# Parting one tile's load so that its last 448 columns go to four of the sixteen DMA engines

## The chip, the cores and the metric

The kernel runs on one core of a Trainium2 chip. The metric is the device time of one execution in microseconds (us). Executions of one kernel agree within some 0.3% as a rule; now and then one is more than 1.5% above the fastest and counts as "slow". A *ratio* below is the mean time of one kernel's fast runs over the mean time of the other's fast runs of the same rounds on the same chip, so it is not quite the ratio of the medians that are quoted beside it.

## The reference

A softmax over groups of 544 neighbouring columns, in float32. The input is 285.2 MB and the output as much.

```python
# x: (4, 4096, 4352) float32, 8 groups of 544 columns
x_g = x.reshape(B, N, G, Dg)
x_g = x_g - x_g.max(axis=-1, keepdims=True)
exp = np.exp(x_g)
out = exp / exp.sum(axis=-1, keepdims=True)
```

## The kernel before

The 16,384 rows make 64 tiles of 128 partitions with two rows each, so a tile is 128 x 8,704 float32, and one partition's row of it is 34,816 B. There are six buffers in SBUF, the on-chip memory. A tile is loaded, its 16 group maxima are taken on DVE (the vector engine), ACT (the scalar engine) computes the exponentials with their sums, DVE takes the reciprocals and scales in place, and the tile is stored from the same buffer. SP (the sync engine) issues the loads, POOL (GpSimd) most of the stores, and a load into a used buffer waits for the store of six tiles earlier:

```python
    for t in range(nt):
        if t >= NT:
            nc.sync.wait_ge(stored[t % NT], 16 * (t // NT))
        tile_in = bufs[t % NT]
        if t < nt - 1:
            nc.sync.dma_start(out=tile_in[:, :], in_=xt[t]).then_inc(landed[t % NT], 16)
        else:
            # ... the last tile (63) is loaded in two halves of columns
    for t in range(nt - LAST, nt):      # LAST = 2: SP also stores tiles 62 and 63
        nc.sync.wait_ge(scaled, t + 1 if t < nt - 1 else len(parts))
        nc.sync.dma_start(out=ot[t], in_=bufs[t % NT][:, :]).then_inc(last_stored, 16)

    for t in range(nt - LAST):          # POOL stores the others
        nc.gpsimd.wait_ge(scaled, t + 1)
        nc.gpsimd.dma_start(out=ot[t], in_=bufs[t % NT][:, :]).then_inc(stored[t % NT], 16)
```

DVE works in a fixed order, in which the max of a tile stands ahead of the scale of the tile before.

```python
    vector_max(0)                       # waits for landed[...]
    for n in range(len(parts)):
        if n + 1 < len(parts):
            vector_max(n + 1)
        vector_scale(n)                 # waits for the exponentials of n
```

Of the kernel before, what the change touches and what calls it, by code (L numbers as in the profile page):

```python
# [1 line left out]

# [4 lines left out]


@with_exitstack
def kernel(  # L10
    ctx: ExitStack,
    tc: tile.TileContext,
    x: bass.AP,
    out: bass.AP,
):
    nc = tc.nc
    G = 8
    P = 128
    R = 2
    NT = 6  # L20
    RG = R * G
    xf = x.flatten_outer_dims()
    of = out.flatten_outer_dims()
    N, D = xf.shape
    Dg = D // G
    nt = N // (P * R)
    LAST = 2
    FIRST = 2
    turns = (nt - 1 - FIRST) // NT
    f32 = mybir.dt.float32  # L30
    X = mybir.AxisListType.X
    Exp = mybir.ActivationFunctionType.Exp
    xt = xf.rearrange("(t p r) d -> t p (r d)", p=P, r=R)
    ot = of.rearrange("(t p r) d -> t p (r d)", p=P, r=R)

    landed = [tc.alloc_semaphore(f"landed{b}") for b in range(NT)]
    stored = [tc.alloc_semaphore(f"stored{b}") for b in range(NT)]
    last_landed = tc.alloc_semaphore("last_landed")
    last_stored = tc.alloc_semaphore("last_stored")


    max_done = tc.alloc_semaphore("max_done")
    exp_done = tc.alloc_semaphore("exp_done")
    rec_done = tc.alloc_semaphore("rec_done")
    scaled = tc.alloc_semaphore("scaled")

    ctx.enter_context(tc.tile_critical(  # L47
        sync_engine=mybir.EngineType.Pool, no_gpsimd_drain=True))
    bufs = [ctx.enter_context(nc.sbuf_tensor(f"xt{b}", [P, R * D], f32)) for b in range(NT)]
    mx = ctx.enter_context(nc.sbuf_tensor("mx", [P, NT, RG], f32))  # L50
    sm = ctx.enter_context(nc.sbuf_tensor("sm", [P, NT, RG], f32))
    rs = ctx.enter_context(nc.sbuf_tensor("rs", [P, NT, RG], f32))

    parts = [(t, slice(0, RG)) for t in range(nt - 1)]
    parts += [(nt - 1, slice(r * G, (r + 1) * G)) for r in range(R)]

    def groups(t, g):
        return bufs[t % NT][:, :].rearrange("p (g d) -> p g d", d=Dg)[:, g, :]

    def vector_max(n):  # L60
        t, g = parts[n]
        i = nc.vector.reduce_max(  # L62
            out=mx[:, t % NT, g], in_=groups(t, g), axis=X, negate=True)
        if g.start == 0:
            i.wait_op(landed[t % NT], 16 * (t // NT + 1), "sem-ge")
        else:
            i.wait_op(last_landed, 16, "sem-ge")
        i.then_inc(max_done, 1)

    def vector_scale(n):  # L70
        t, g = parts[n]
        nc.vector.reciprocal(out=rs[:, t % NT, g], in_=sm[:, t % NT, g]).wait_op(  # L72
            exp_done, n + 1, "sem-ge").then_inc(rec_done, 1)
        xg = groups(t, g)
        nc.vector.tensor_tensor(  # L75
            out=xg,
            in0=xg,
            in1=rs[:, t % NT, g].unsqueeze(2).to_broadcast([P, g.stop - g.start, Dg]),
            op=mybir.AluOpType.mult,
        ).wait_op(rec_done, n + 1, "sem-ge").then_inc(scaled, 1)  # L80

    def scalar_exp(n, count):
        t, gs = parts[n]
        xg = groups(t, gs)
        for g in range(gs.start, gs.stop):
            i = nc.scalar.activation(  # L86
                out=xg[:, g - gs.start, :],
                in_=xg[:, g - gs.start, :],
                func=Exp,
                bias=mx[:, t % NT, g:g + 1],  # L90
                scale=1.0,
                accum_out=sm[:, t % NT, g:g + 1],
            )
            if g == gs.start:
                i.wait_op(max_done, count, "sem-ge")
        i.then_inc(exp_done, 1)



    for t in range(nt):  # L100
        if t >= NT:
            nc.sync.wait_ge(stored[t % NT], 16 * (t // NT))
        tile_in = bufs[t % NT]
        if t < nt - 1:
            nc.sync.dma_start(out=tile_in[:, :], in_=xt[t]).then_inc(landed[t % NT], 16)  # L105
        else:
            for r in range(R):
                nc.sync.dma_start(
                    out=tile_in[:, r * D:(r + 1) * D], in_=xt[t, :, r * D:(r + 1) * D],
                ).then_inc(landed[t % NT] if r < R - 1 else last_landed, 16)  # L110
    for t in range(nt - LAST, nt):
        nc.sync.wait_ge(scaled, t + 1 if t < nt - 1 else len(parts))
        nc.sync.dma_start(out=ot[t], in_=bufs[t % NT][:, :]).then_inc(last_stored, 16)


    for t in range(nt - LAST):
        nc.gpsimd.wait_ge(scaled, t + 1)
        nc.gpsimd.dma_start(out=ot[t], in_=bufs[t % NT][:, :]).then_inc(stored[t % NT], 16)  # L118
    for t in range(nt - NT, nt - LAST):
        nc.gpsimd.wait_ge(stored[t % NT], 16 * (t // NT + 1))  # L120
    nc.gpsimd.drain()
    nc.gpsimd.wait_ge(last_stored, 16 * LAST)

    nc.scalar.preload_act_table(Exp)  # L124

    for n in range(FIRST):
        scalar_exp(n, n + 1)
    nc.scalar.sem_inc(max_done, -FIRST)
    with nc.scalar.Fori(0, turns):
        for k in range(NT):  # L130
            scalar_exp(FIRST + k, k + 1)
        nc.scalar.sem_inc(max_done, -NT)
    for k, n in enumerate(range(FIRST + turns * NT, len(parts))):
        scalar_exp(n, k + 1)


    vector_max(0)
# [3 lines that stand above are left out]
        vector_scale(n)  # L141


# [1 line left out]
_INS = ['x']  # L145
_OUTS = [((4, 4096, 4352), 'float32')]


# [23 lines left out]
```

## Time and profile before

| | before |
|---|---|
| median of the runs | 1326.43 us (1326.30 to 1326.44) |
| span in the profile | 1324.7 us |
| moved | 570.48 MB at 431 GB/s |
| DVE / ACT busy | 90% / 57% |

The prediction below shows the main lines of the page and of the timeline. Beside them, the table by stretches from 1220 to 1320 us is of use. Its columns are the stretch, its length, the busy time of DVE, ACT and POOL with the count of their instructions, a clock that is of no interest here, the busy share of the 16 DMA engines, and GB/s.

```profile
1220.00:1260.00 40.00, 35.95 (x7) 23.63 (x64) 1.07 (x2) 1.00 1.00 430
1260.00:1280.00 20.00, 19.97 (x4) 11.82 (x32) 0.53 (x1) 1.00 1.01 433
1280.00:1300.00 20.00, 19.56 (x6) 11.14 (x31) 0.00 (x0) 1.00 1.01 436
1300.00:1320.00 20.00, 4.90 (x2) 0.78 (x3) 0.00 (x0) 1.00 0.99 427
```

The DMA engines are fully busy to the very end, also after DVE has finished at 1305.7 us: the last stores still wait in line. The times to landing of the two stores that SP issues (minimum, median, maximum) say the same:

```profile
L113 SPq DMA_DIRECT2D out_dram<-xt x2: 343/346/348, 1290.2 to 1305.8; - x2
...
DMA to landing us min/median/max: 17.5/20.1/22.8
```

The last store, issued at 1305.8 us, needs 17.5 us although its rows take only 10.3 us: it stands behind the rows of tile 62.

### The profile page before, as it was taken

Reading aid. Unit: us, or ns where it says so; the run is one execution under the profiler, and the core shown is the slowest. Engines: PE = TensorE matmul, PEld = TensorE weight load, DVE = VectorE, ACT = ScalarE, POOL = GpSimd, SP = SyncE. Lnnn points to the kernel's source line nnn. Section 1 sums busy time; section 2 is a strip of 40 time slices with the busy share of each in tenths; the row PEclk is TensorE's granted clock in tenths of the full one; section 3 lists DMA queues with packets and bytes.
Section 4 is the critical chain, followed back from the end, with each engine's and each line's share of the span. In section 5 each row is a group of like instructions: output and inputs, shape, how many; then the busy total and the mean of one; then the engine's idle time right before and its main releaser. Section 6 shows DMA issues by size and latency. Waiting matters only on the chain.

```text
span 1324.7 us, 2465 instructions
## 1 busy us (share of the span) xinstructions
DVE 1190.0 (90%) x195; ACT 757.4 (57%) x2049; POOL 33.3 (3%) x66
## 2 busy tenths in 40 slices
DVE  5999999988989889898898998988989889898893
ACT  3765566547456465564655646556465474654751
POOL 0000000000000000000000000000000000000000
DMA  9999999999999999999999999999999999999998
GB/s 404 421 434 433 432 432 434 434 432 431 435 435 432 430 434 437 432 432 432 436 434 430 433 435 433 431 433 435 433 433 431 434 436 432 431 432 437 432 432 372
DMA packets 18582, 570.48 MB, mean 431 GB/s; under 512 B 2064, under 2 KB 2064, under 8 KB 2064
## 3 DMA queue, kind: packets, MB, share of 16 engines
q1 hardware_dynamic: 9648, 294.13, 51.5%
q0 software_dynamic: 8928, 276.30, 48.3%
q14 instruction: 6, 0.05, 0.0%
HBM read 285.21 MB, written 285.21 MB: 431 GB/s over the span
## 4 chain that ended last, share of the span: by engine, by line
another core or an unknown queue 69%; DVE 20%; DMA 7%; ACT 1%; SPq 1%; issue 0%; POOLq 0%
DVE xt L75 10%; DVE mx L62 10%; DMA out_dram<-xt 4%; DMA xt<-in_x_dram 3%; ACT xt L86 1%; SPq L105 1%; DVE rs L72 0%; SPq L167 0%; POOLq L47 0%; POOLq L156 0%
## 5 line engine op out<-in xcount | busy, mean ns | idle before, releaser
L86 ACT ACTIVATE xt<-xt,mx 128x544 f32<-128x544 f32 x1024 | 750.1, 734 | 542.4 <-DVE mx L62 542.4
L62 DVE TENSOR_REDUCE mx<-xt 128x16 f32<-128x8704 f32 (+1 forms) x65 | 590.1, 9079 | 110.8 <-DMA xt<-in_x_dram 110.8
L75 DVE TENSOR_TENSOR xt<-xt,rs 128x8704 f32<-128x8704 f32 (+1 forms) x65 | 590.6, 9086 | 2.2
L86 ACT ACTIVATION_READ_ACCUMULATOR xt<-xt,mx 128x1 f32 x1024 | 191.6, 187 | 0.0
L118 POOL DMA_DIRECT2D out_dram<-xt x62 | 33.1, 534 | 1243.5 <-DVE xt L75 1243.5
L72 DVE RECIPROCAL rs<-sm 128x16 f32<-128x16 f32 (+1 forms) x65 | 15.7, 242 | 2.8 <-ACT xt L86 2.8
L124 ACT ACT_TABLE_LOAD x1 | 1.3, 1283 | 0.9 <-PEq L156 0.9
L156 POOL MEMSET const-float32-0.0<- 128x1 f32 x1 | 0.1, 98 | 0.2 <-issue 0.2
L156 POOL MEMSET const-bfloat16-1.0<- 128x1 bf16 x1 | 0.1, 101 | 0.0
L156 POOL MEMSET const-uint8-127<- 128x1 uint8 x1 | 0.1, 99 | 0.0
L156 POOL MEMSET const-float32-1.0<- 128x1 f32 x1 | 0.1, 98 | 0.0
## 6 DMA issues: line engine op xcount, KB each, us to landing
xt<-in_x_dram SPq DMA_DIRECT2D x63, 4352.0 KB, 32.4
out_dram<-xt POOLq DMA_DIRECT2D x62, 4352.0 KB, 51.5
out_dram<-xt SPq DMA_DIRECT2D x2, 4352.0 KB, 20.1
xt<-in_x_dram SPq DMA_DIRECT2D x2, 2176.0 KB, 35.1
```

What stands on the lines that cost most here:

```text
L62: i = nc.vector.reduce_max(out=mx[:, t % NT, g], in_=groups(t, g), axis=X, negate=True)
L72: nc.vector.reciprocal(out=rs[:, t % NT, g], in_=sm[:, t % NT, g]).wait_op(exp_done, n + 1, "sem-ge").then_inc(rec_done, 1)
L75: nc.vector.tensor_tensor(out=xg, in0=xg, in1=rs[:, t % NT, g].unsqueeze(2).to_broadcast([P, g.stop - g.start, Dg]), op=mybir.AluOpType.mu ...
L86: i = nc.scalar.activation(out=xg[:, g - gs.start, :], in_=xg[:, g - gs.start, :], func=Exp, bias=mx[:, t % NT, g:g + 1], scale=1.0, accum ...
L105: nc.sync.dma_start(out=tile_in[:, :], in_=xt[t]).then_inc(landed[t % NT], 16)
L118: nc.gpsimd.dma_start(out=ot[t], in_=bufs[t % NT][:, :]).then_inc(stored[t % NT], 16)
L124: nc.scalar.preload_act_table(Exp)
L156: nc = _bacc.Bacc("TRN2", target_bir_lowering=False, num_devices=1)
```

## The change

The load of tile 61 is parted. The main DMA takes all but the last 448 columns of all 128 partitions. Two more DMAs take those columns for 124 and for 4 partitions. 124 and 4 look chosen because each runs on four engines, where 128 partitions run on 16: the prediction cites the rule for this. The intent, as far as the code tells it, is to take a little work off twelve engines and to give it to four. The wait of the max of tile 61 counts two more DMAs.

```diff
+    PARTED, COL, RANGES = 61, R * D - 448, [124, 4]
@@ vector_max
         if g.start == 0:
-            i.wait_op(landed[t % NT], 16 * (t // NT + 1), "sem-ge")
+            more = 16 * len(RANGES) if t >= PARTED and t % NT == PARTED % NT else 0
+            i.wait_op(landed[t % NT], 16 * (t // NT + 1) + more, "sem-ge")
@@ the loads
-        if t < nt - 1:
+        if t == PARTED:
+            nc.sync.dma_start(out=tile_in[:, :COL], in_=xt[t, :, :COL]).then_inc(
+                landed[t % NT], 16)
+            p = 0
+            for size in RANGES:
+                nc.sync.dma_start(
+                    out=tile_in[p:p + size, COL:], in_=xt[t, p:p + size, COL:],
+                ).then_inc(landed[t % NT], 16)
+                p += size
+        elif t < nt - 1:
             nc.sync.dma_start(out=tile_in[:, :], in_=xt[t]).then_inc(landed[t % NT], 16)
```

## The prediction

> **What bounds the kernel now.** I read the page first (engine shares, the 40 slices, the DMA queues), then the DMA issues, the waits of the DMA queue, the chain of work that ended last, the timeline of DVE, POOL and SP over the last 130 us, and last the trace's single packet records. The page and the waits of SP:
>
> ```profile
> DVE 1190.0 (90%) x195; ACT 757.4 (57%) x2049; POOL 33.3 (3%) x66
> DMA  9999999999999999999999999999999999999998
> GB/s 404 421 434 433 432 432 434 434 432 431 435 435 432 430 434 437 432 432 432 436 434 430 433 435 433 431 433 435 433 433 431 434 436 432 431 432 437 432 432 372
> q1 hardware_dynamic: 9648, 294.13, 51.5%
> q0 software_dynamic: 8928, 276.30, 48.3%
> ...
> SPq L105 <- DMA out_dram<-xt: 1201.7, 57, 67.8
> ```
>
> The reader is to see that the DMA is full from the first slice to the last, at some 433 GB/s: 570.4 MB at that rate are 1317 us of the 1324.7 us span. Loads are on q1 (issued by SP, line 105), stores on q0 (issued by POOL, line 118), and SP's only large wait is for a store to free a buffer. DVE, at 90%, is next. In the steady part a tile takes 20.6 us and DVE works 18.6 us of them (max 9.1, reciprocal 0.2, scale 9.2, gaps), so its slack is 2 us a tile. The timeline shows this for tiles 60 to 63, with the stores of tiles 58 to 61 beside it:
>
> ```profile
> 1214.59 0.53 POOL L118 DMA_DIRECT2D out_dram<-xt  x1 [20.07 <-DVE xt L75]
> 1235.21 0.53 POOL L118 DMA_DIRECT2D out_dram<-xt  x1 [20.10 <-DVE xt L75]
> 1255.82 0.53 POOL L118 DMA_DIRECT2D out_dram<-xt  x1 [20.08 <-DVE xt L75]
> 1276.47 0.53 POOL L118 DMA_DIRECT2D out_dram<-xt  x1 [20.11 <-DVE xt L75]
> ...
> 1216.28 9.22 DVE L62 TENSOR_REDUCE mx<-xt 128x16 f32<-128x8704 f32 x1 [1.99 <-DMA xt<-in_x_dram]
> 1236.89 9.22 DVE L62 TENSOR_REDUCE mx<-xt 128x16 f32<-128x8704 f32 x1 [1.97 <-DMA xt<-in_x_dram]
> 1246.30 9.22 DVE L75 TENSOR_TENSOR xt<-xt,rs 128x8704 f32<-128x8704 f32 x1
> 1257.54 9.22 DVE L62 TENSOR_REDUCE mx<-xt 128x16 f32<-128x8704 f32 x1 [2.01 <-DMA xt<-in_x_dram]
> 1290.22 15.90 SPq L113 DMA_DIRECT2D out_dram<-xt  x2
> ```
>
> The max at 1236.89 is that of tile 61 and waits for its load. DVE's program has max(61) ahead of scale(60), so a late tile 61 also holds back the store of tile 60, issued at 1255.82. After max(62) at 1257.54 DVE waits for no more loads: from there the tail is a chain of DVE work up to the last store's issue (the second of line 113, 1305.78 by its record), and the rows of that store run 10.3 us on every engine.
>
> **The packet records.** One row of a tile (34,816 B) is one record, and each DMA engine takes one after the other without a gap, so the 16 engines can be threaded by matching ends to starts. One engine's thread around the load of tile 63, which comes in half rows (start us, queue, bytes):
>
> ```
> 1255.74 q1 17408    1256.39 q0 34816
> 1257.67 q1 17408    1258.32 q0 34816
> 1259.60 q1 17408    1260.25 q0 4
> 1260.25 q1 17408    1260.90 q0 34816
> ```
>
> Two things follow. Cost: a whole row holds the engine 1.285 us, a half row 0.645 us, so a record costs about 5 ns plus 36.8 ns per 1000 B. Order: the engine alternates between q0 and q1 **record by record, whatever their size**. A half row waits a full store row for its turn, and even the 4-byte semaphore record at the end of a DMA uses up a turn. The engines' last records end between 1319.8 and 1322.8 us, 14 of the 16 by 1321.5.
>
> **What the Trainium skill says.** "DMA: Bandwidth & Descriptors", section "Why a DMA increments its semaphore by 16 and not by 1": a DMA uses the largest k up to 16 that divides the outer dimension, on the lowest-numbered engines if issued from SP. 124 and 4 both give k = 4; 31 rows and 1 row on each of engines 0 to 3. The trace before has only k = 16 and cannot confirm it. Same page, "Queues, rings and completion order": an engine round-robins between queues at packet granularity, of some 9 to 17 descriptors. The trace agrees with the turns but not the size: here a turn is one row. Same page, "Rules for kernel authors": a smaller k confines a DMA to fewer engines.
>
> **The change, part by part.**
> 1. The main load of tile 61 has rows of 33,024 B: 8 rows times 1,792 B times 36.8 ns/KB = 0.53 us less work on every engine.
> 2. Engines 0 to 3 get 32 rows of 1,792 B, each 5 + 66 = 71 ns: 2.28 us more, net +1.75 us. Were throughput all, the end would move by -0.5 us (the two latest engines not among the four: they end 1.3 us after the rest) or up to +1.75 us.
> 3. The turns. The main rows of tile 61 end on the engines at about 1232.7 to 1236.4 us (semaphore records of that load). On engines 0 to 3 the 32 short rows then come one per store turn as long as stores are queued. Queued are, by the thread shown, 3 rows of the store of tile 57, 8 of 58 and 8 of 59 (issued 1235.2): 19 rows and 3 semaphores, so 22 short rows go between them and the last 10 follow at once. 19 x 1.285 + 32 x 0.071 = 26.7 us. The store of tile 60 cannot join, as it hangs on max(61). So tile 61 lands 26.7 us after some 1233.4, at 1260 instead of 1236.4; max(61) starts near 1260.8, **23.9 us late**.
> 4. From there DVE runs without waiting (tiles 62 and 63 have landed by its turn): max(61) 9.15, reciprocal 0.17, scale(60) 9.23 -> store 60 at 1279.4 (was 1255.8). Max(62) and scale(61), 18.55 -> store 61 at 1297.9 (was 1276.5). First half max of 63, 4.6, with scale(62), 9.4 -> store 62 at 1311.9 (was 1290.2). Then 15.56, as before -> the last store at 1327.5 (was 1305.8). So the last store is 21.7 us late: DVE gets back the 2 us that it used to wait for tile 62.
> 5. The DMA hides a little of that. Before, the last store's rows queued behind those of tile 62 until 1309.5 to 1312.5; afterwards the engines have run dry (each has some 45 us of rows left at 1233, which end before store 60 is issued). It starts 1 us (as the first load: issued 0.9, first record 1.9) to 2.6 us after issue, needs 10.3 us of rows, and 1.9 us pass from the last record to the end of the span, as now. End of span: 1327.5 + 1 to 2.6 + 10.3 + 1.9 = 1340.7 to 1342.3; the measured time is 1.8 us above the span: 1342.5 to 1344.1. This is +16 to +18 us, 1.3%.
>
> **Rivals.** (a) Throughput alone: short rows cost only their bytes. For it: the change looks meant for this, giving work to engines with spare time at the end; if the hardware takes many short rows in one turn, as the page's 9 to 17 descriptors would have it, 32 rows need 2 to 4 turns, 3 to 5 us, of which DVE gets 2 back. Then 1326 to 1330. Against it: the 4-byte records use whole turns. I give this 20%. (b) The four engines include the late ones or the stores queue is longer: load 61 then lands near 1263 and the time is 1345 to 1347. (c) DVE or ACT becomes the bound: between 1260 and 1327 it is DVE, which is already in step 4. (d) The delay is hidden by six buffers: against it, at 1245 SP has issued its last load, so later loads can't use the gap, and each later store needs DVE in order.
>
> **Range and chances.** Steps 3 to 5 with 75 to 80%: 1342 to 1347. Rival (a): 1326 to 1330. I say 1342.5, range 1326 to 1347. 2% is 26.5 us: above 1353 would need a delay of 34 us or so, more than the queued stores can give; below 1300 is out of reach, as 1317 us is pure transfer.
>
> **What the profile would show.** The short rows: 128 records of 1,792 B, on q1, each following a store row on four threads between 1233 and 1260; wrong if they run in bursts. The wait of max(61) for its load about 26 us instead of 2.0. Stores by POOL at 1279 and 1298 where 1256 and 1276 were. DMA share well under 9 tenths in the last two slices. If max(61) is late by under 5 us, step 3 is wrong; if it is late by 24 and the end is not, step 5 is.

## The result

The changed kernel takes 1344.94 us in the median (1344.59 to 1345.08 in three fast runs; a fourth, at 1367.28 us, was slow and is left out). Before takes 1326.43 us. The ratio is 1.0139, with a 95% interval of 1.0119 to 1.0159: 18.5 us more, which is within 2%. The profiled run is a fast one; its span is 1342.8 us.

The page of the changed kernel, in its busy tenths and rates:

```profile
DVE  5999999998988988989989889899898898897395
DMA  9999999999999999999999999999999999999966
GB/s 399 431 431 431 432 431 434 438 435 432 434 431 434 431 431 436 437 435 432 431 432 432 431 431 437 438 432 432 431 435 431 431 435 437 435 432 428 428 278 299
```

For 38 slices nothing has changed. In the last two the DMA falls to 6 tenths, where before it was at 9 and 8. The timeline of DVE, POOL and SP shows the cause (start, length, instruction, and in brackets the idle time before it):

```profile
1216.35 9.22 DVE L66 TENSOR_REDUCE mx<-xt 128x16 f32<-128x8704 f32 x1 [1.98 <-DMA xt<-in_x_dram]
1225.76 9.23 DVE L80 TENSOR_TENSOR xt<-xt,rs 128x8704 f32<-128x8704 f32 x1
1262.90 9.22 DVE L66 TENSOR_REDUCE mx<-xt 128x16 f32<-128x8704 f32 x1 [27.92 <-DMA xt<-in_x_dram]
1272.32 9.22 DVE L80 TENSOR_TENSOR xt<-xt,rs 128x8704 f32<-128x8704 f32 x1
1281.46 9.21 DVE L66 TENSOR_REDUCE mx<-xt 128x16 f32<-128x8704 f32 x1
...
1235.28 0.53 POOL L132 DMA_DIRECT2D out_dram<-xt  x1 [20.09 <-DVE xt L80]
1281.84 0.53 POOL L132 DMA_DIRECT2D out_dram<-xt  x1 [46.02 <-DVE xt L80]
1300.39 0.53 POOL L132 DMA_DIRECT2D out_dram<-xt  x1 [18.02 <-DVE xt L80]
...
1314.13 15.90 SPq L127 DMA_DIRECT2D out_dram<-xt  x2
```

The max of tile 61 (1262.90) waits 27.9 us for its load where it waited 2.0 us. The store of tile 60, which comes after it in DVE's order, is issued at 1281.84 us and not at 1255.82 us. The max of tile 62 (1281.46) then waits for nothing, so the 2 us that it used to wait are won back, and every later store is some 24 us late: the last one is issued at 1329.69 us by its record (1314.13 is the first of the pair) and not at 1305.78 us.

The same stretches as shown of before:

```profile
1220.00:1260.00 40.00, 14.95 (x3) 11.82 (x32) 0.53 (x1) 1.00 0.99 427
1260.00:1280.00 20.00, 17.06 (x3) 7.84 (x21) 0.00 (x0) 1.00 0.94 403
1280.00:1300.00 20.00, 19.96 (x4) 13.27 (x37) 0.53 (x1) 1.00 0.54 232
1300.00:1320.00 20.00, 19.93 (x7) 9.74 (x27) 0.53 (x1) 1.00 0.78 335
1320.00:1340.00 20.00, 8.43 (x3) 4.70 (x14) 0.00 (x0) 1.00 0.78 334
```

The stall of DVE between 1235 and 1263 us costs the DMA next to nothing while it lasts (share 0.99): there are rows in the queues. The bill comes after, from 1260 to 1340 us, when the engines have emptied their queues and wait for stores: 20 x (0.06 + 0.46 + 0.22 + 0.22) = 19.2 us of idle engines, against 18.5 us of longer time.

The records of single packets show what held up the load. This is one engine's thread, found by matching each record's end with the next one's start (start us, length ns, queue, bytes; here q0 carries stores and q1 loads; 4 bytes are the semaphore record that ends a DMA on an engine; lines are left out at the dots):

```
1234.501    74  q1   1792
1234.571  1288  q0  34816
1235.856    74  q1   1792
1235.926  1288  q0  34816
1237.211    74  q1   1792
1237.282     9  q0      4
1237.288    74  q1   1792
...
1257.764  1578  q0  34816
1259.338   280  q1   1792
1259.615     9  q0      4
1259.620   261  q1   1792
1259.878    74  q1   1792
1259.949    74  q1   1792
```

A short row takes 74 ns and then gives the engine to a store row of 1,288 ns. Between the first and the last short row 18 store rows pass. Only when the stores are used up, at 1259.6 us, do the last short rows follow each other. There are 128 records of 1,792 B; the first starts at 1234.50 us, the last at 1262.07 us. That four engines do this can also be read from the semaphore records of 4 bytes, one per engine of a DMA: there are 2,072 of them against 2,064, so the two added DMAs have 8 between them, and after the short rows these come in four pairs (1260.5, 1261.0, 1261.8 and 1262.1 us): each DMA ran on the same four engines. The records do not name the engines, so that they are the lowest four is not shown.

### The profile page after: what moved, and what is told of

It is laid out like the page before. It is cut to its first block, busy times and chain, and to the rows that moved or that the text cites. A ratio compares the mean times of both kernels' runs of the same rounds, so it can differ in the third digit from the quotient of the medians.

```text
span 1342.8 us, 2467 instructions
## 1 busy us (share of the span) xinstructions
DVE 1189.9 (89%) x195; ACT 757.4 (56%) x2049; POOL 33.4 (2%) x66
## 2 busy tenths in 40 slices
DMA packets 18718, 570.48 MB, mean 425 GB/s; under 512 B 2072, under 2 KB 2200, under 8 KB 2200
## 4 chain that ended last, share of the span: by engine, by line
another core or an unknown queue 65%; DVE 24%; DMA 7%; ACT 1%; SPq 1%; issue 0%; POOLq 0%
DVE xt L80 12%; DVE mx L66 12%; DMA out_dram<-xt 4%; DMA xt<-in_x_dram 3%; ACT xt L91 1%; SPq L119 1%; DVE rs L77 0%; SPq L181 0%; POOLq L51 0%; POOLq L170 0%
## 6 DMA issues: line engine op xcount, KB each, us to landing
out_dram<-xt SPq DMA_DIRECT2D x2, 4352.0 KB, 11.7
```

## The experiments

The theory: *each short row waits for one store row as long as stores are queued; the load lands late by that; the delay passes through DVE's order to the last store.* The rivals: the loss is the 43 KB more that four engines carry; it is a fixed price of more DMAs and semaphores; it is a price per short row without limit; it is only the store of tile 60 that is held back. All ten runs gave correct results. The edits are shown against the changed kernel. "max(61)" below is the max of tile 61.

### All engines

```diff
-    PARTED, COL, RANGES = 61, R * D - 448, [124, 4]
+    PARTED, COL, RANGES = 61, R * D - 448, [128]
```

> The same 448 columns of tile 61 in one further DMA of 128 partitions, so all 16 engines get 8 short rows each and none has more bytes than another. Theory of the turns (each short row waits for one store row while stores are queued): 8 turns, 8 x 1.356 = 10.8 us, so the max of tile 61 starts 10 to 11 us later than before (near 1247.5 us), the last store is issued some 8.6 us later, of which the queue of the tail hides some: 1329 to 1331 us. Rival of the bytes (the four engines' 43 KB more are the loss): no loss is left, 1326 to 1327 us, the max of tile 61 waits about 2.5 us. Rival of the added DMA and its semaphore alone (fixed cost): the same 18 us as the change, 1344 us, or half of it with one DMA in place of two, 1335 us.

Measured: 1331.09 us (1330.96 to 1331.21) against 1326.63 us, ratio 1.0029 (1.0013 to 1.0046). The waits in its timeline:

```profile
1247.23 9.22 DVE L66 TENSOR_REDUCE mx<-xt 128x16 f32<-128x8704 f32 x1 [12.33 <-DMA xt<-in_x_dram]
1267.84 9.22 DVE L66 TENSOR_REDUCE mx<-xt 128x16 f32<-128x8704 f32 x1 [1.97 <-DMA xt<-in_x_dram]
```

max(61) starts 10.3 us later than before, for 8 short rows on each engine, with no imbalance of bytes at all. The rival of the bytes falls (it said 1326 to 1327 us), and so does the fixed price (1335 or 1344 us). The theory's range was missed by 0.1 us, for a reason that the second line shows: DVE still waits 1.97 us for tile 62, so the 2 us that I had counted as won back are not. By its last semaphore record the load of tile 62 landed at 1267.4 us against 1257.0 us before, as much later as that of tile 61. In the change it landed at 1272.4 us, but there max(61) was late by 26 us and hid this.

### Narrow columns

```diff
-    PARTED, COL, RANGES = 61, R * D - 448, [124, 4]
+    PARTED, COL, RANGES = 61, R * D - 64, [124, 4]
```

> The change with 64 columns in place of 448: 32 short rows on each of four engines as before, but of 256 B. Theory of the turns: as many turns, so the max of tile 61 starts some 1.8 us earlier than in the change (32 x 66 ns x 6/7), near 1261 us, and the time is 1342.5 to 1344 us. Rival of the bytes: a seventh of the loss, 1326 to 1329 us.

Measured: 1344.37 us (1344.07 to 1345.61), ratio 1.0132 (1.0115 to 1.0149); max(61) at 1262.39 us after a wait of 27.40 us. The time is 0.4 us above the range of the theory and far from that of the rival. With a seventh of the bytes the loss is 17.7 us against 18.5 us: the bytes hardly matter and the rows do. max(61) moved by only 0.5 us against the change, less than the 1.8 us expected. The records account for about as much: the short rows start up to 0.5 us later (1236.4 against 1235.95 us on the last engine, behind main rows that are longer by 1,536 B), and on that engine six of the last store rows, at 1,301 to 2,136 ns, took 1.8 us more than 1,288 ns each, where in the change one, at 2,074 ns, took 0.8 us more. Why they were stretched is not shown.

### Two engines

```diff
-    PARTED, COL, RANGES = 61, R * D - 448, [124, 4]
+    PARTED, COL, RANGES = 61, R * D - 448, [62, 62, 4]
```

> Ranges of 62, 62 and 4 partitions: two engines get 63 short rows each, two others 1. Theory of the turns, capped by the stores that are queued (19 rows of the stores of tiles 57 to 59; the store of tile 60 hangs on this very load): the first 22 rows or so take turns, the other 41 follow at once, so the landing is only 31 x 71 ns = 2.2 us later than in the change: max of tile 61 near 1265 us, time 1346 to 1348 us. Rival without the cap (each short row costs one store row, 63 x 1.356 = 85 us): max of tile 61 near 1320 us, time about 1400 us.

Measured: 1346.92 us in the median of four runs (1346.56 to 1355.84, all counted as fast), ratio 1.017 (1.0134 to 1.0206, so it is unclear whether this is over 2%). The profile (of a run at 1346.78 us):

```profile
1264.96 9.22 DVE L66 TENSOR_REDUCE mx<-xt 128x16 f32<-128x8704 f32 x1 [29.96 <-DMA xt<-in_x_dram]
```

Twice the short rows on an engine cost 2.1 us more (2.2 expected), not another 26 us. The price is limited by the store rows that happen to be queued: 19 by the prediction, 18 by the change's records.

### Tile 30 and tile 57

```diff
-    PARTED, COL, RANGES = 61, R * D - 448, [124, 4]
+    PARTED, COL, RANGES = 30, R * D - 448, [124, 4]    # and 57 in another run
```

> The same parting at tile 30 in place of 61: same bytes, same rows, stores queued in the same way. Theory: the load lands 26 to 28 us late there too and the max of tile 30 waits about 28 us, but the loads of the next tiles keep the engines at work meanwhile and DVE regains 2 us a tile over some 12 tiles, so the DMA never runs dry at the end: 1326.4 to 1328.5 us. Rival (a stall of DVE of 26 us costs its length less 2 us plus tail slack wherever it falls, because DMA time lost is never regained): 1340 to 1345 us.

Measured: 1327.70 us (1327.18 to 1328.39) against 1326.63 us, ratio 1.0003 (0.9987 to 1.002).

```profile
588.05 9.23 DVE L80 TENSOR_TENSOR xt<-xt,rs 128x8704 f32<-128x8704 f32 x1
625.10 9.22 DVE L66 TENSOR_REDUCE mx<-xt 128x16 f32<-128x8704 f32 x1 [27.83 <-DMA xt<-in_x_dram]
...
838.55 9.23 DVE L80 TENSOR_TENSOR xt<-xt,rs 128x8704 f32<-128x8704 f32 x1
848.51 9.22 DVE L66 TENSOR_REDUCE mx<-xt 128x16 f32<-128x8704 f32 x1 [0.74 <-DMA xt<-in_x_dram]
869.07 9.22 DVE L66 TENSOR_REDUCE mx<-xt 128x16 f32<-128x8704 f32 x1 [1.92 <-DMA xt<-in_x_dram]
```

The stall is the same, 27.83 us, and it costs nothing that can be told from the spread. Between 643 and 829 us there are eleven maxima without a wait; the first with one is at 848.51 us, and at 869.07 us DVE waits its usual 1.9 us again. In that time DVE went at its own 18.55 us a tile and not at the DMA's 20.6 us.

> The parting at tile 57, four tiles earlier. Theory of the stall that DVE pays back at 2 us a tile: four more tiles give back 8 us of the 18.5 us: 1336 to 1338 us. Rival (the loss is a property of the stall and not of its place): 1344 to 1345 us. Rival (any place but the very last is free): 1326 to 1328 us.

Measured: 1335.55 us (1335.23 to 1335.94) against 1326.53 us, ratio 1.0063 (1.0049 to 1.0078). The max of tile 57 waits 27.43 us, and the five tiles 58 to 62 follow without a wait. The last store is issued at 1321.0 us, 15.2 us late, where four tiles later it was 23.9 us late: 8.7 us, or 2.2 us a tile. The time is 0.5 us below the range expected (1336 to 1338 us) and far from both rivals.

```profile
1179.97 9.22 DVE L66 TENSOR_REDUCE mx<-xt 128x16 f32<-128x8704 f32 x1 [27.43 <-DMA xt<-in_x_dram]
...
L127 SPq DMA_DIRECT2D out_dram<-xt x2: 343/346/348, 1305.4 to 1321.0; - x2
...
DMA to landing us min/median/max: 11.7/11.7/11.7
```

So the loss is one of place: a stall of this kind is repaid at some 2 us a tile, and only what the tiles left cannot repay is lost.

### Scale ahead of the late max

```diff
-        if n + 1 < len(parts):
+        if n + 1 < len(parts) and n + 1 != PARTED:
             vector_max(n + 1)
         vector_scale(n)
+        if n + 1 == PARTED:
+            vector_max(n + 1)
```

> The change, with DVE's scale of tile 60 put ahead of its max of tile 61, so that the store of tile 60 is no longer held back by the late load. Theory of the turns: that store joins the queue on the four engines near 1246 us and gives the last 10 short rows 8 more store rows to wait for, 8 x 1.285 = 10.3 us: the max of tile 61 starts near 1272 us, later than in the change (1262.9), and though one scale is then done already (9.4 us), the exp of tile 61 has nothing to hide under: 1345 to 1349 us, no better than the change. Rival (the loss is the store of tile 60 held back): about 10 us or more is regained, 1327 to 1335 us.

Measured: 1348.97 us (1348.39 to 1349.63), ratio 1.0167 (1.0152 to 1.0182). This is slower than the change, by about 4 us.

```profile
1273.29 9.22 DVE L66 TENSOR_REDUCE mx<-xt 128x16 f32<-128x8704 f32 x1 [26.39 <-DMA xt<-in_x_dram]
...
1247.19 0.53 POOL L132 DMA_DIRECT2D out_dram<-xt  x1 [11.44 <-DVE xt L80]
1304.19 0.53 POOL L132 DMA_DIRECT2D out_dram<-xt  x1 [56.47 <-DVE xt L80]
```

The store of tile 60 is issued at 1247.19 us, no longer held back. Its 8 rows on each of the four engines give the short rows 8 more turns to wait for, 10.3 us (the records have 26 or 27 store rows between an engine's short rows, where the change has 18), and max(61) moves from 1262.90 to 1273.29 us, by 10.4 us. This is the sharpest sign of the turns: an earlier store makes the load later. The rival that blamed the held-back store falls.

### Tile 3

```diff
-    PARTED, COL, RANGES = 61, R * D - 448, [124, 4]
+    PARTED, COL, RANGES = 3, R * D - 448, [124, 4]
```

> The same parting at tile 3, whose load runs before any store is queued. Theory of the turns: with no stores there are no turns to wait for, the 128 short rows run in bursts of 32 x 71 ns, the load lands within some 2 us of its old time, and DVE does not wait for it. What is left is the 1.75 us of further work on four engines: 1325.9 us if the engine that ends last is not one of the four, up to 1328.4 us if it is. Rival (short rows cost a turn by themselves, or the semaphores do): the wait of the max of tile 3 grows by 20 us or more.

Measured: 1329.16 us (1328.68 to 1331.20) against 1326.53 us, ratio 1.002 (1.0007 to 1.0033). The 128 short rows run between 43.4 and 47.6 us, before the first store record at 49.9 us, and DVE does not wait for tile 3. So without stores there are no turns to pay for. What is left, 2.6 us, is above the 1.75 us of further work that I had worked out for the four engines, and 0.8 us above the range expected. The 71 ns a row were too low here: the short rows had a median of 121 ns and a mean of 115 ns, and only 24 of the 128 took 74 ns. So 32 of them are some 3.7 us in place of 2.28 us (an estimate from the mean), less the 0.53 us saved. Why they take longer here is not shown. The last records end at 1323.9 to 1325.4 us on five engines and at 1321.8 to 1321.9 us on eleven, so a few engines do end late; why it is five and not four I can't tell from the records.

### Tries for a better version

If four engines with more work end late, then less work on the engine that ends last should help. 120 partitions run on 15 engines and 8 on 8, by the rule, which leaves the sixteenth with less (the rule is the one that the prediction cites).

```diff
-    PARTED, COL, RANGES = 61, R * D - 448, [124, 4]
+    PARTED, COL, RANGES = 3, R * D - 1792, [120, 8]    # early120
+    PARTED, COL, RANGES = 3, R * D - 448, [120, 8]     # early120_narrow
+    PARTED, COL, RANGES = 3, R * D - 1792, [128]       # early_even
```

> For a better version: at tile 3, before stores are queued, the last 1,792 columns go in DMAs of 120 and 8 partitions, which by the rule of the largest divisor run on 15 and 8 engines: the sixteenth engine loses 8 x 7,168 B = 2.1 us of work, eight engines get 0.26 us more. If the engine that ends last (1.3 us behind the rest in the trace before) is the sixteenth, the time falls by 1 to 2 us, to 1324.5 to 1325.5 us; if it is another, the time is 1326.2 to 1327 us.

Measured: 1335.30 to 1354.39 us in four fast runs and 1355.41 and 1356.95 us in two slow ones, ratio of the fast runs 1.0109 (1.0065 to 1.0152). The expectation failed. The count of semaphore records (2,087, which is 2,064 + 15 + 8) fits DMAs on 15 and 8 engines. The only profile is of a slow run. In it 1,403 whole-row records are longer than 1.3 us, against 119 in the profile of before; since that is a slow run, it explains nothing of the fast ones.

> The try for a better version gave 1335 to 1357 us, with load records stretched over 1.3 us on every engine through the whole run, which no theory here foresaw. This one shifts a quarter of that (448 columns at tile 3, in DMAs of 120 and 8 partitions: 0.53 us less work on one engine, 0.07 us more on eight). If any unequal shift ahead of the steady part brings the stretched records: 1329 us or more and hundreds of records over 1.3 us after the first 100 us. If only a shift of 2 us or so does: 1325.8 to 1327 us.

Measured: 1326.65, 1326.72 and 1327.23 us in three runs and 1332.23, 1334.47 and 1334.73 us in three others; ratio 1.0034 (1.0014 to 1.0053). The profile is of a run at 1326.72 us, with 135 whole-row records over 1.3 us, about as many as before.

> Control for that: 1,792 columns of tile 3 in one further DMA of 128 partitions, so no engine has more work than another and all get 8 rows of 7,168 B more. If the unequal work is what upsets the steady part: 1326.2 to 1327 us, as before. If the split load itself does (rows of 27,648 and 7,168 B ahead of the steady part), the time is 1330 us or more here too.

Measured: 1326.40 to 1327.30 us in five runs and 1339.85 us in one; ratio 1.0024 (0.9995 to 1.0052). 140 such records in its profile, of a run at 1326.40 us.

The best runs of both are level with before (1326.42 us) and none beats it. Some runs are 6 to 13 us longer, even with equal work on all engines (the run of two engines at 1355.84 us, 9 us above its fellows, may be another), and none of those was profiled. So neither the unequal work nor the split load is shown to be the cause; that stays open. No version of this idea was found that beats the kernel before.

## Why the prediction was right

The time of 1344.94 us lies in the range of 1326 to 1347 us, 2.4 us above the 1342.5 us named as likeliest and 0.8 us above the band of 1342.5 to 1344.1 us of the fifth step, whose lower edge it named. The range alone proves little, since it also holds the 1326 to 1330 us of rival (a); what bears the prediction out is the mechanism, which came as described. By its steps:

1. **Less work on all engines, more on four.** The sizes hold: main rows of 33,024 B took 1,222 ns and short rows 74 ns, the latter 71 ns from start to start as worked out (in tile 3 they took longer). As a cause they hardly count (narrow columns: 0.8 us less loss for six sevenths fewer bytes).
2. **The turns.** Right, and shown five ways: by the records, by 8 rows on all engines, by 64 columns in place of 448, by the limit with two engines, and by the earlier store that makes the load later.
3. **The size of the delay.** Predicted max(61) at 1260.8 us, measured 1262.9 us. The mis-sized term is the start of the short rows: I took 1233.4 us, and on the four engines they began at 1234.5 to 1235.95 us. The load lands with the last of the four, so this term was 2.55 us too early; the run of the short rows from there was 26.1 us, with 18 store rows, in place of 26.7 us with 19.
4. **DVE's chain.** Predicted 21.7 us of delay for the last store, measured 23.9 us; the 2.2 us are those of step 3. The chain itself is as worked out: one wait of 2 us is won back and no more.
5. **What the tail hides.** Predicted a start of 1 to 2.6 us after issue; the records of the last store's rows begin 0.8 to 1.0 us after it, at or under the low end. This makes up for part of the 2.2 us of step 4, which is a piece of luck in the number. The last store landed 11.7 us after its issue where it took 17.5 us before, so 5.8 us are hidden. The figure is about the same in every variant that left the queues dry at the end:

| run | last store issued later by, us | time longer by, us | hidden, us |
|---|---|---|---|
| the change | 23.9 | 18.5 | 5.4 |
| all engines | 10.3 | 4.5 | 5.8 |
| narrow columns | 23.4 | 17.7 | 5.7 |
| two engines | 26.0 | 20.3 | 5.7 |
| tile 57 | 15.2 | 9.0 | 6.2 |
| scale first | 27.7 | 22.4 | 5.3 |

(The issue of the last store is taken from the traces, against 1305.78 us before; the time is the difference of the medians.)

Of the rivals, (a), throughput alone, at 20%, fell with all engines and narrow columns. (b), a later landing on the same path, is what the 2 us of step 3 amount to. (c), DVE as the bound, is no separate rival: DVE was busy for 19.96 of the 20 us from 1280 to 1300 us, as step 4 has it. (d), a delay hidden by the six buffers, was rejected for the reason that no later tiles are left to use the gap; tile 30 shows that this reason was the right one, since there the same stall is hidden whole.

## What to carry to other kernels

Where two queues share the DMA engines, count the turns and not the bytes: here a short row, of 1,792 or of 256 B, beside queued rows of 34,816 B waited for one of them, 1,285 ns, so a load should not be cut into many short rows while large stores are waiting. A stall in a kernel bound by its transfers can be free, as at tile 30, if the queues hold enough to bridge it and the other engines have slack to catch up before the end: multiply the slack of a tile (here 2 us) by the tiles that are left. Near the end most of the same stall is paid: 18.5 of 26 us at tile 61.

## What the Trainium skill lacked or had wrong

- "DMA: Bandwidth & Descriptors", section "Queues, rings and completion order", says that an engine takes turns between queues at the granularity of a packet, typically of some 9 to 17 descriptors. In these traces a turn was one row, whatever its size: a row of 1,792 B (74 ns), one of 256 B (18 ns) and even a 4-byte semaphore record alternated with store rows of 34,816 B (1,288 ns).
- The same page, section "Rules for kernel authors", warns that a smaller k confines a DMA to fewer engines, but not what that costs beside another full queue: 32 short rows on each of four engines made a load land 26 us late, 8 on each of sixteen 10 us late. The rule for k that the prediction took from this page was borne out for 124 and 4 partitions (four pairs of semaphore records, so four engines each), and the count for 120 and 8 fits 15 and 8 engines (23 more records).
- "Perfetto Trace Analysis", section "DMA Optimizations", says that small DMAs under 2 KB have a significant overhead per transfer. It speaks of whole DMAs, and the rows of 1,792 B here are parts of a DMA of 217 KB, so it is not tested here. What the section lacks is the turn: such a row waited 1,285 ns beside queued stores, where the last ones followed each other every 71 ns.
- No page tells of executions that come out 6 to 13 us longer in a kernel whose other executions take 1326 to 1327 us, as with the parted load of tile 3; the cause is open.
